# Six of the twelve modulation sums of each layer computed beside the mixer's first projections, the others moved from routing into the pair stage

## The chip, the cores and the metric

The kernel runs on one core of one Trainium2 chip, in one launch. The metric is the device time of the launch in microseconds (us). A launch of the kernel before takes 3448.68 us (median of three, 3448.21 to 3457.46). The execution that was profiled took 3438.13 us, of which the trace spans 3436.4 us. PE is the matrix engine, PEld its weight loads, DVE the vector engine, ACT the scalar engine, POOL the GpSimd engine and SP the engine that issues nearly all DMAs.

## The reference

The program is a two-layer trunk over 512 tokens of width 1024. Each layer is a mixer and a feed-forward part with product-key experts, both in float32, and both are steered by a vector `c` of the sequence:

```python
for l in range(DEPTH):
    mod = c_act @ ada_w[l] + ada_b[l]                 # 6144 numbers
    sh1, sc1, g1, sh2, sc2, g2 = jnp.split(mod, 6, axis=-1)
    h = modulate(rmsnorm(x, ln1_g[l]), sh1, sc1)      # h * (1 + sc1) + sh1
    proj = h @ w_full
    r, k, v, wd, ad, gd = ...                         # token shift, split
    y_rwkv = rwkv7_mix(...)                           # a recurrence over tokens
    y_pool = multiscale_pool(...)
    x = x + g1 * (concatenate([y_rwkv, y_pool]) @ w_out[l])
    h2 = modulate(rmsnorm(x, ln2_g[l]), sh2, sc2)
    x = x + g2 * peer_ffn(h2, ...)                    # 16 queries, top 16, experts
return rmsnorm(x, lnf_g)
```

`mod` is a product of one vector with a matrix of 1024 x 6144. The kernel computes it in 12 groups of 512 columns per layer: groups 0 to 3 are `sh1` and `sc1`, 4 and 5 are `g1`, 6 to 9 are `sh2` and `sc2`, and 10 and 11 are `g2`. So a layer's groups 0 to 3 are wanted before its mixer begins, 4 and 5 before its output projection, 6 to 9 before its queries, and 10 and 11 at the layer's end.

## The kernel before, in words

**A group's sum.** A group reads 2 MB of `ada_w`. DVE multiplies eight tiles of 128x512 by a column each and adds them up (one TENSOR_SCALAR, L195, and seven SCALAR_TENSOR_TENSOR, L197, in `ada_acc`). `ada_mod` then sums the accumulator over its partitions with four matmuls of one column (L205) into a PSUM tile of the ring `pss`, which has two slots, and DVE adds the bias (L207). Four of the groups also cost a tiny `mod_scale` on DVE.

**Where the tiles land.** With `early=True` the group's data come as eight loads of 256 KB into general buffers (L183). Otherwise they come as four loads of 512 KB into the ring `raw` (L185), which has three buffers. The same ring carries the weights: `split_next` loads a weight tile into `raw` (L257), ACT copies its upper part (L259), DVE subtracts to get the lower part (L260), and `mm3` runs three passes of eight matmuls with the two parts. Weights are split three tiles ahead of their use. SP issues loads in program order, so a load that waits for a buffer holds up the loads behind it.

**The stages of a layer.** The mixer projects tile 12, the four k tiles 4 to 7, then four r tiles, tile 13, four v tiles and four pooled tiles (`shifted` evacuates the first ten; L384 on ACT, L385 on DVE). Between them come decay, normalisation and the scaled keys (`at`, L435 and following), whose products go through DRAM into `Ai`. A triangular solve on DVE (L479 to L484) turns `Ai` into `Fi`, and the result goes through DRAM into `Fb`. The pair stage begins where `Fb` is first used (L644): chunks of the recurrence for four pairs of heads, with a chain of small steps between PE and DVE (L706 to L708), ending in the output projection. Then the feed-forward part runs 16 query projections (evacuated on ACT, L916), each followed by scores whose best 16 are found on DVE (L903 to L908, L930). The rest of routing sorts out experts, and one-hot products (L1044) and the dense expert loops follow.

**Who sets the order.** A scheduler fixes each engine's order of instructions before the launch, starting from the order of the calls. `zipped` and `blend` deal out lists of steps among each other. `tc.issue_after(x)` keeps what is called within it behind the instruction `x` on the same engine; nothing else binds these sums to a place.

**Where the sums stand.** `ADA_MIX` names those in the pair stage (three of its `zipped` calls carry `ada` steps). `ADA_PRE` names those among the queries and scores: every second query starts one of its list with `early=True`. Groups 0 to 3 of layer 0 are summed at the very start of the program, and no edit touches them.

Of the kernel before, what the change touches and what calls it, by code (L numbers as in the profile page):

```python
# [9 lines left out]
F32 = mybir.dt.float32  # L10
# [4 lines left out]
AF = mybir.ActivationFunctionType  # L15
ALU = mybir.AluOpType
# [3 lines left out]
P = 128  # L20
T = 512
# [3 lines left out]
L = 2  # L25
# [9 lines left out]
SPILL = 88  # L35
GPRE = 24
GFRAC = 0.0
ADA_MIX = [[(l, g) for g in range(4, 10)] for l in range(L)]
ADA_PRE = [[(0, 10), (0, 11), (1, 0), (1, 1), (1, 2), (1, 3)], [(1, 10), (1, 11)]]
ADA_DENSE = [[], []]  # L40
SIDES, NPRE = (0, 8, 0, 3), 2
APER, AOFF, ADEL = 2, 1, 4
# [66 lines left out]
def body(ctx, tc, A, tap=None):  # L109
    nc = tc.nc  # L110
    V, S, G, TE = nc.vector, nc.scalar, nc.gpsimd, nc.tensor
# [3 lines left out]
    st = ctx.enter_context(tc.tile_pool(name="st", bufs=3))  # L115
# [7 lines left out]
    def nm(p):  # L123
        cnt[0] += 1
        return f"{p}{cnt[0]}"
# [3 lines left out]
    def bank(shape=(P, T)):  # L129
        return psp[0].tile(list(shape), F32, tag="ps", name=nm("ps"))  # L130

    def sbank(shape=(P, T)):
        return pss.tile(list(shape), F32, tag="pss", name=nm("pss"))

    def s2t(name, shape=(P, T), dt=F32):
        return s2.tile(list(shape), dt, tag="s2", name=nm(name))
# [6 lines left out]
    sc_ = pers.tile([P, ND], F32, name="silu_c")  # L143
# [5 lines left out]
    def C(n):  # L149
        o, w = COFF[n]  # L150
        return const[:, o:o + w]
# [21 lines left out]
    A2 = [pers.tile([P, ND], F32, name=f"A2_{l}") for l in range(L)]  # L173

    first = {}

    def ada_acc(l, g, side=0, early=False):
        acc = s2t("acc")
# [23 lines left out]
    def ada_mod(l, g, acc):  # L202
        pt = sbank((P, 4))
        for m in range(4):
            TE.matmul(pt[:, m:m + 1], acc[:, m * P:(m + 1) * P], C("one"), start=True, stop=True)  # L205
        o = VOFF["adab"][0]
        V.tensor_tensor(mods[l][:, 4 * g:4 * g + 4], pt, vecs[l][:, o + 4 * g:o + 4 * g + 4], op=ALU.add)  # L207
        if g in (2, 3, 8, 9):
            mod_scale(l, 1 if g < 6 else 2, g % 2)
# [21 lines left out]
    def vec(l, n, i=0, w=1):  # L231
        o = VOFF[n][0]
        return vecs[l][:, o + i:o + i + w]

    def mod_scale(l, which, half):
        a, ln, off = (A1, "ln1", 8) if which == 1 else (A2, "ln2", 32)
        o = 4 * half
        V.scalar_tensor_tensor(a[l][:, o:o + 4], mods[l][:, off + o:off + o + 4], 1.0, vec(l, ln, o, 4), op0=ALU.add, op1=ALU.mult)
# [24 lines left out]
    def weights(*key):  # L263
        i = taken[0]
        assert seq[i] == key, (seq[i], key)
        taken[0] += 1
        while len(ready) < min(i + WAHEAD, len(seq)):
            split_next()
        w, ready[i] = ready[i], None
        return w  # L270
# [47 lines left out]
    def mixer(l):  # L318
        with ExitStack() as mctx:
# [26 lines left out]
            omu = m.tile([P, 15], F32, name="omu")  # L346
# [24 lines left out]
            def project(n):  # L371
                if n in begun:
                    w, pt = begun.pop(n)
                    mm3(pt, w, hs, range(ND // 2, ND), start=False)
                    return pt
                w = weights(f"w_in{l}", n)
                pt = sbank()
                mm3(pt, w, hs)
                return pt

            def shifted(n, out):
                pt = project(n)
                mi = n if n < 14 else 14
                S.activation(out, pt, AF.Identity, scale=omu[:, mi:mi + 1])  # L384
                V.scalar_tensor_tensor(out[:, 1:], pt[:, :T - 1], vec(l, "mu", mi), out[:, 1:], op0=ALU.mult, op1=ALU.add)  # L385
                return out

            def c3(z):
# [2 lines left out]
            def n3(z):  # L391
                return z.rearrange("p (n t) -> p n t", n=NT)

            lora = shifted(12, s2t("lora"))
            wda = s2t("wda")
            V.memset(wda[64:65, :], 1.0)
            S.activation(wda[0:64], lora[0:64], AF.Tanh)
            sig = []
            for t in range(NT):
                pt = bank()  # L400
# [4 lines left out]
            for p in range(4):  # L405
                pt = bank()
                TE.matmul(pt, sm[64:128, SM_AUP + p * P:SM_AUP + (p + 1) * P], lora[64:128], start=True, stop=True)
                bt_[p] = s2t("bt")
                S.activation(bt_[p], pt, AF.Sigmoid, bias=vec(l, "a0", p))
            ks = [shifted(4 + p, s2t("k")) for p in range(4)]  # L410

            Pds, kps = [], ks
# [23 lines left out]
            for p in range(4):  # L436
                k, a, at, Pd, Pi = ks[p], bt_[p], at_[p], Pds[p], kt_[p]
# [312 lines left out]

            todo, accs = ADA_MIX[l], {}

            def ada_step(i):
                if i > 0:
                    ada_mod(*todo[i - 1], accs.pop(i - 1))
                if i < len(todo):
                    with tc.issue_after(beat[0].ins):
                        accs[i] = ada_acc(*todo[i])

            ada = [lambda i=i: ada_step(i) for i in range(len(todo) + 1)]  # L760
# [24 lines left out]
            for n in range(ND):  # L785
                xr = s2t("x")
                nc.sync.dma_start(xr, A["xT"][:, n] if l == 0 else xs[n])
                if n in held:
                    w, pt = held.pop(n)
                    mm3(pt, w, ys, (3,), True, start=False)  # L790
                else:
                    w, pt = weights("w_out", l, n), (sbank, bank)[n % 2]()
# [10 lines left out]
            pt = sbank((P, 2, NT))  # L803
# [10 lines left out]
    def peer(l):  # L814
        with ExitStack() as pctx:
# [73 lines left out]
            with ExitStack() as rctx:  # L889
# [159 lines left out]

                pre = list(ADA_PRE[l])  # L1050
                for hp in range(16):
# [204 lines left out]
    for l in range(L):  # L1256
        mixer(l)
        peer(l)
# [56 lines left out]
```

## Time and profile before

| what | value |
|---|---|
| median of three launches | 3448.68 us |
| the profiled execution | 3438.13 us |
| its span in the trace | 3436.4 us |
| mean granted PE clock | 0.952 of full speed |
| PE busy | 3211.2 us (93%) |
| DVE busy | 2809.3 us (82%) |
| ACT busy | 1386.0 us (40%) |
| modulation loads in the ring `raw` | 48 of 512 KB |
| modulation loads in general buffers | 96 of 256 KB |

The profiled execution is 10.55 us below the median, and 10.08 us below the fastest of the three launches. Busy shares are averages over stages that have different limits, so the profile is read by stretches. In layer 0 the front of the mixer is 62.0 to 225.3 us, the pair stage 225.3 to 442.5, the queries with their scores 442.5 to 577.8, the rest of routing 577.8 to 677.1, and the first part with one-hot products 677.1 to 1002.9. In layer 1 the same stretches begin at 1741.6, 1922.1, 2139.1, 2255.7 and 2356.4 us. The pair stage is read below up to 422.5 and 2119.0 us; what follows it up to the first query is the norm of the second half.

### The profile page before, as it was taken

How to read it: one execution, taken by the hardware profiler on the slowest of the kernel's cores; microseconds unless marked ns; L12 is line 12 of the kernel's file. 1: busy time of each engine (PE TensorE's matmuls, PEld its weight loads, DVE VectorE, ACT ScalarE, POOL GpSimd, SP SyncE). 2: the span in 40 equal slices, each digit the busy share in tenths (PEclk: the TensorE clock that was granted, in tenths of full speed). 3: DMA queues.
4: the chain of work that ended last, by engine and by line, in shares of the span. 5: the costliest groups of instructions: out<-in, count | busy, mean ns of one | idle time of the engine just before them, and what ended most of it. 6: DMA issues, size and time to landing. Idle time of an engine off the chain costs nothing. (4 is left out here: it accounts for less than half of the span.)

```text
span 3436.4 us, 51106 instructions
## 1 busy us (share of the span) xinstructions
PE 3211.2 (93%) x18154; PEld 2814.1 (82%) x18154; DVE 2809.3 (82%) x6227; ACT 1386.0 (40%) x2228; POOL 875.7 (25%) x684
## 2 busy tenths in 40 slices
PE   5889888999999999999899898999999999999997
PEld 3777678999998888888777777889999888888886
DVE  5677499989868888899939675999997688888998
ACT  3433222446563334333353323334656533333333
POOL 2000001432202222555500000023240122245564
PEclk7989899999999999999999888999999999999998
DMA  5214253567789999999922233345767999999996
GB/s 196 77 47 144 88 176 122 171 228 257 262 310 344 345 343 342 350 377 398 356 72 82 79 111 117 99 134 180 275 237 282 333 334 343 342 340 335 362 392 237
DMA packets 361377, 826.41 MB, mean 240 GB/s; under 512 B 46496, under 2 KB 189600, under 8 KB 357792
## 3 DMA queue, kind: packets, MB, share of 16 engines
q1 hardware_dynamic: 287392, 554.68, 47.5%
q0 software_dynamic: 73728, 268.47, 20.8%
q8 instruction: 142, 2.33, 0.3%
q14 instruction: 115, 0.94, 0.1%
HBM read 730.75 MB, written 92.27 MB: 240 GB/s over the span
## 5 line engine op out<-in xcount | busy, mean ns | idle before, releaser
L277 PE MATMUL pss<-hi,wsp 128*128 128x384 f32 (+1 forms) x5168 | 1081.5, 360 | 88.4 <-DVE wsp L260 27.8
L1162 PE MATMUL ps<-vv,wg 128*128 128x512 f32 x4608 | 1077.3, 392 | 22.7 <-DVE vv L1146 6.9
L277 PEld LDWEIGHTS pss<-hi,wsp 128*128 128x128 f32 x5168 | 941.0, 195 | 162.8 <-DVE wsp L260 39.9
L1162 PEld LDWEIGHTS ps<-vv,wg 128*128 128x128 f32 x4608 | 866.0, 189 | 208.0 <-ACT vv L1145 10.4
L259 ACT ACTIVATE wsp<-raw 128x1024 fp32r<-128x1024 f32 x341 | 360.0, 1057 | 548.5 <-PE pss L277 428.9
L277 PE MATMUL pss<-lo,wsp 128*128 128x384 f32 (+1 forms) x2584 | 534.1, 347 | 0.0
L855 POOL DMA_INDIRECT row<-u,ex x256 | 318.8, 1245 | 837.1 <-DVE row L861 639.5
L260 DVE TENSOR_TENSOR wsp<-raw,wsp 128x1024 fp32r<-128x1024 f32 x341 | 432.4, 1269 | 69.9 <-ACT wsp L259 69.7
L277 PEld LDWEIGHTS pss<-lo,wsp 128*128 128x128 f32 x2584 | 461.4, 188 | 22.2 <-issue 0.5
L855 POOL DMA_INDIRECT row<-v,ex x256 | 336.3, 1314 | 244.5 <-DVE ox L869 190.6
L1146 DVE TENSOR_TENSOR vv<-raw,vv 128x512 fp32r<-128x512 f32 x512 | 345.4, 692 | 43.1 <-ACT vv L1145 39.3
L1145 ACT ACTIVATE vv<-raw 128x512 fp32r<-128x512 f32 x512 | 291.4, 619 | 111.5 <-DMA raw<-v 76.9
L1136 ACT ACTIVATE wg<-ge 128x384 fp32r<-128x384 f32 x256 | 132.9, 524 | 497.6 <-DVE ge L1134 206.3
L861 DVE SCALAR_TENSOR_TENSOR row<-row,hx 128x1024 f32<-128x1024 f32 x256 | 318.4, 1250 | 14.0 <-DMA row<-u,ex 14.0
L869 DVE SCALAR_TENSOR_TENSOR ox<-row,wx,ox 128x1024 f32<-128x1024 f32 x254 | 325.3, 1281 | 2.4
L971 POOL TENSOR_TENSOR eq<-eq,cid 128x400 f32<-128x400 f32 x128 | 181.7, 1439 | 478.8 <-DVE eq L969 341.1
L937 POOL TENSOR_TENSOR hf<-hi,lo 128x128 f32<-128x128 f32 x16 | 7.8, 503 | 925.6 <-DVE tw L906 450.4
L1137 DVE TENSOR_TENSOR wg<-ge,wg 128x384 fp32r<-128x384 f32 x256 | 141.3, 555 | 104.6 <-ACT wg L1136 93.9
L1046 ACT ACTIVATE gb<-ps 128x512 f32<-128x512 f32 x192 | 199.0, 1161 | 0.0
L1134 DVE TENSOR_TENSOR ge<-ge,g 128x192 f32<-128x192 f32 x496 | 157.0, 353 | 46.3 <-DMA g<-gscr 39.3
L1129 ACT ACTIVATE ge<-pss 128x384 f32<-128x384 f32 x80 | 39.2, 490 | 249.0 <-PE pss L277 243.1
L1025 DVE TENSOR_TENSOR oh<-oh,selg 128x1024 f16<-128x1024 f16 x96 | 71.2, 742 | 44.9 <-PE ps L1044 44.7
(459 smaller groups left out, 3194.5 us busy)
## 6 DMA issues: line engine op xcount, KB each, us to landing
raw<-uT SPq DMA_DIRECT2D x256, 512.0 KB
raw<-v SPq DMA_DIRECT2D x256, 512.0 KB
gscr<-gb SPq DMA_DIRECT2D x24, 2048.0 KB
g<-gscr SPq DMA_DIRECT2D x124, 384.0 KB
gespill<-ge SPq DMA_DIRECT2D x176, 192.0 KB
ge<-gespill SPq DMA_DIRECT2D x176, 192.0 KB
ada<-ada SPq DMA_DIRECT2D x96, 256.0 KB
raw<-ada SPq DMA_DIRECT2D x48, 512.0 KB
```

Of the source, the lines that this page charges most:

```text
L259: S.activation(w[:, 0], raw, AF.Copy)
L260: V.tensor_tensor(w[:, 1], raw, w[:, 0].bitcast(F32), op=ALU.subtract)
L277: TE.matmul(pt, w[:, a, k * P:(k + 1) * P], hs[k][b], start=start and n == 0, stop=stop and n == len(steps) - 1)
L855: G.indirect_dma_start(out=rows[n], out_offset=None, in_=A["u" if n < P else "v"], in_offset=bass.IndirectOffsetOnAxis(ap=ex[:, n % P:n % ...
L861: V.scalar_tensor_tensor(row, row, 1.0, hx, op0=ALU.mult, op1=ALU.mult, accum_out=dots[:, e:e + 1])
L869: V.scalar_tensor_tensor(ox, row, wx[:, e:e + 1], ox, op0=ALU.mult, op1=ALU.add)
L971: pace["G"] = G.tensor_tensor(eq, eq, z["id"][:, h].unsqueeze(1).to_broadcast([P, 8, NC]), op=ALU.mult)
L1046: S.activation(gb[:, :, o:o + 4].rearrange("p i t -> p t i"), pt, AF.Copy, scale=1.0 / GSC)
L1134: V.tensor_tensor(gq, gq, g[:, :, c % IG], op=ALU.mult)
L1145: S.activation(vv[0][q], raw[:, q * T:(q + 1) * T], AF.Copy)
L1146: vlo[q] = V.tensor_tensor(vv[1][q], raw[:, q * T:(q + 1) * T], vv[0][q].bitcast(F32), op=ALU.subtract)
L1162: end[0] = TE.matmul(acc[t][d2], wg[a][:, ts_], vv[b][d2], start=(c == 0 and a == 0 and b == 0), stop=(c == NK - 1 and a == 1))
```

## The change

Groups 4 to 9 of each layer go from the pair stage into `ADA_FRONT`. `ada_parts` cuts each group into five steps: four quarters (one load of 512 KB into the ring `raw` and two operations on DVE each) and `ada_mod`. That makes 30 steps per layer. `shifted` evacuates a projection and then calls `FSTEPS` = 3 of them, held behind its own evacuation on ACT, which binds none of the engines that the steps use. The ten calls of `shifted` for tiles 12, 4 to 7, 0 to 3 and 13 therefore use up the 30 steps. The places in the pair stage take over what stood among the scores: six groups in layer 0 (its own 10 and 11, and 0 to 3 of layer 1), and two in layer 1. Routing gets none. The number of groups, their operations and their bytes stay as they were; eight groups that used loads of 256 KB now use loads of 512 KB in the ring.

```diff
-ADA_MIX = [[(l, g) for g in range(4, 10)] for l in range(L)]
-ADA_PRE = [[(0, 10), (0, 11), (1, 0), (1, 1), (1, 2), (1, 3)], [(1, 10), (1, 11)]]
+ADA_FRONT = [[(l, g) for g in range(4, 10)] for l in range(L)]
+ADA_MIX = [[(0, 10), (0, 11), (1, 0), (1, 1), (1, 2), (1, 3)], [(1, 10), (1, 11)]]
+ADA_PRE = [[], []]
+FSTEPS = 3
...
+    def ada_parts(l, g):
+        accs = []
+
+        def quarter(q):
+            if q == 0:
+                accs.append(s2t("acc"))
+            w = st.tile([P, 2, T], F32, tag="raw", name=nm("raw"))
+            nc.sync.dma_start(w, A["ada"][l, g, q])
+            for kk in range(2):
+                k = 2 * q + kk
+                if k == 0:
+                    V.tensor_scalar(accs[0], w[:, kk], sc_[:, k:k + 1], None, op0=ALU.mult)
+                else:
+                    V.scalar_tensor_tensor(accs[0], w[:, kk], sc_[:, k:k + 1], accs[0], op0=ALU.mult, op1=ALU.add)
+
+        return [lambda q=q: quarter(q) for q in range(4)] + [lambda: ada_mod(l, g, accs[0])]
...
+            front = [f for lg in ADA_FRONT[l] for f in ada_parts(*lg)]
+
             def shifted(n, out):
                 pt = project(n)
                 mi = n if n < 14 else 14
-                S.activation(out, pt, AF.Identity, scale=omu[:, mi:mi + 1])
+                begin = S.activation(out, pt, AF.Identity, scale=omu[:, mi:mi + 1])
                 V.scalar_tensor_tensor(out[:, 1:], pt[:, :T - 1], vec(l, "mu", mi), out[:, 1:], op0=ALU.mult, op1=ALU.add)
+                with tc.issue_after(begin.ins):
+                    for _ in range(FSTEPS):
+                        if front:
+                            front.pop(0)()
                 return out
```

The lines move down by up to 25: the sums of the front stand at L186 (load), L190 and L192 (DVE) afterwards, L257 becomes L276, L260 becomes L279, L479 and L480 become L504 and L505, and L903 to L906 become L928 to L931.

On SP, the issue order in layer 0 before the solve, just ahead of and behind the first `acmp` store to DRAM. Before:

```order
L257 DMA raw_981<-w_in 128x1024
L257 DMA raw_1023<-w_in 128x1024
L257 DMA raw_1066<-w_in 128x1024
L465 DMA ascr_124<-acmp_646 32x16x32 x4
L257 DMA raw_1109<-w_in 128x1024
L257 DMA raw_1150<-w_in 128x1024
L465 DMA ascr_124<-acmp_647 32x16x32 x4
```

The same place after:

```order
L186 DMA raw_903<-ada 128x1024
L186 DMA raw_907<-ada 128x1024
L186 DMA raw_911<-ada 128x1024
L490 DMA ascr_124<-acmp_715 32x16x32 x4
L276 DMA raw_929<-w_in 128x1024
L490 DMA ascr_124<-acmp_716 32x16x32 x4
L186 DMA raw_961<-ada 128x1024
L186 DMA raw_972<-ada 128x1024
L493 DMA Ai<-ascr_124 128x1024
```

The loads of the sums now take two or three buffers of the ring between two weight tiles, and two of them stand ahead of the load of `Ai`.

On DVE, the small rows of the solve in layer 0 (`Fi`, `Ai`), with the splits of weights (`wsp`) among them. Before:

```order
L479 TENSOR_TENSOR prod<-Fi,Ai 128x36 x2
L480 TENSOR_REDUCE Fi<-prod 128x6 x2
L479 TENSOR_TENSOR prod<-Fi,Ai 128x49 x2
L480 TENSOR_REDUCE Fi<-prod 128x7 x2
L479 TENSOR_TENSOR prod<-Fi,Ai 128x64 x2
L480 TENSOR_REDUCE Fi<-prod 128x8 x2
L260 TENSOR_TENSOR wsp_1152<-raw_1150,wsp_1152 128x1024
```

The same rows after:

```order
L279 TENSOR_TENSOR wsp_988<-raw_986,wsp_988 128x1024
L504 TENSOR_TENSOR prod<-Fi,Ai 128x36 x2
L192 SCALAR_TENSOR_TENSOR acc_971<-raw_1018,silu_c,acc_971 128x512
L505 TENSOR_REDUCE Fi<-prod 128x6 x2
L192 SCALAR_TENSOR_TENSOR acc_971<-raw_1018,silu_c,acc_971 128x512
L504 TENSOR_TENSOR prod<-Fi,Ai 128x49 x2
L192 SCALAR_TENSOR_TENSOR acc_971<-raw_1022,silu_c,acc_971 128x512
L505 TENSOR_REDUCE Fi<-prod 128x7 x2
L192 SCALAR_TENSOR_TENSOR acc_971<-raw_1022,silu_c,acc_971 128x512
L504 TENSOR_TENSOR prod<-Fi,Ai 128x64 x2
```

Where the steps of the solve followed each other, an operation of a sum now stands between them.

On DVE, the first score of layer 0, where `sc` are a query's scores. Before:

```order
L197 SCALAR_TENSOR_TENSOR acc_3342<-ada_3349,silu_c,acc_3342 128x512
L903 MAX SV_3260<-sc_3372 128x8
L197 SCALAR_TENSOR_TENSOR acc_3342<-ada_3350,silu_c,acc_3342 128x512
L904 MAX_INDEX si_3374<-SV_3260,sc_3372 128x8
L906 MATCH_REPLACE tw_3377<-SV_3260,sc_3372 128x128
L903 MAX SV_3261<-sc_3372 128x8
```

The same place after:

```order
L928 MAX SV_3400<-sc_3487 128x8
L929 MAX_INDEX si_3489<-SV_3400,sc_3487 128x8
L931 MATCH_REPLACE tw_3492<-SV_3400,sc_3487 128x128
L928 MAX SV_3401<-sc_3487 128x8
```

The operations of the sums are gone from between the scores.

## Rows read from the trace of the kernel before

**Rows 1.** The page: busy time, share and instructions of each engine.

```profile
PE 3211.2 (93%) x18154; PEld 2814.1 (82%) x18154; DVE 2809.3 (82%) x6227; ACT 1386.0 (40%) x2228; POOL 875.7 (25%) x684
```

**Rows 2.** Windows by stage: start:end, length, busy of each engine, PEclk, DMA share, GB/s.

```profile
62.00:225.30 163.30, 143.82 (x730) 116.29 (x730) 110.46 (x225) 68.19 (x115) 0.00 (x0) 0.91 0.26 75
225.30:422.50 197.20, 182.70 (x1476) 150.27 (x1474) 124.47 (x277) 62.12 (x128) 0.00 (x0) 0.85 0.30 97
442.50:577.80 135.30, 119.10 (x593) 102.35 (x593) 133.01 (x663) 38.88 (x55) 3.93 (x8) 0.92 0.44 145
577.80:677.10 99.30, 94.40 (x532) 91.35 (x531) 95.02 (x307) 37.41 (x50) 49.89 (x33) 1.00 0.55 165
...
1741.60:1922.10 180.50, 164.75 (x784) 130.31 (x784) 125.47 (x248) 74.98 (x125) 0.00 (x0) 0.90 0.23 70
1922.10:2119.00 196.90, 180.53 (x1474) 148.29 (x1473) 124.51 (x277) 62.01 (x128) 0.00 (x0) 0.88 0.30 97
2139.10:2255.70 116.60, 109.58 (x551) 94.06 (x551) 112.78 (x626) 38.21 (x55) 3.83 (x8) 0.96 0.31 97
2255.70:2356.40 100.70, 96.56 (x543) 95.08 (x541) 93.06 (x305) 37.40 (x50) 42.04 (x33) 0.98 0.54 163
```

**Rows 3.** The score stretches, sums' operations alone: busy of DVE, ACT, POOL.

```profile
442.50:577.80 135.30, 33.47 (x48) 0.00 (x0) 0.00 (x0) 0.92 0.44 145
2139.10:2255.70 116.60, 11.29 (x16) 0.00 (x0) 0.00 (x0) 0.96 0.31 97
```

**Rows 4.** Timeline of ACT, late queries of layer 1: start, duration, operation, idle before.

```profile
2219.88 0.60 ACT L916 ACTIVATE qT<-pss 128x512 f32<-128x512 f32 x1 [4.38 <-PE pss L277]
...
2226.23 0.60 ACT L916 ACTIVATE qT<-pss 128x512 f32<-128x512 f32 x1 [4.32 <-PE pss L277]
```

**Rows 5.** The sums' operations by line: duration in ns, min/median/max.

```profile
L197 DVE SCALAR_TENSOR_TENSOR acc<-raw,silu_c,acc x84: 700/745/753, 256.5 to 2043.8; 128x512 f32<-128x512 f32 x84
...
L195 DVE TENSOR_SCALAR acc<-raw,silu_c x12: 476/481/487, 253.5 to 2037.1; 128x512 f32<-128x512 f32 x12
```

**Rows 6.** Windows of DVE alone in the fronts, parted at the first `at`.

```profile
66.08:121.46 55.38, 16.38 (x23) 0.95 0.19 57
121.46:216.92 95.46, 89.09 (x193) 0.90 0.33 94
1750.92:1806.59 55.67, 16.68 (x24) 0.97 0.18 57
1806.59:1911.65 105.06, 97.55 (x207) 0.90 0.31 91
```

**Rows 7.** Timeline of DVE about the solve of layer 0.

```profile
144.69 2.35 DVE L260 TENSOR_TENSOR wsp<-raw,wsp 128x1024 fp32r<-128x1024 f32 x2
...
158.63 0.23 DVE L479 TENSOR_TENSOR prod<-Fi,Ai 128x1 f32<-128x1 f32 x2 [4.60 <-DMA Ai<-ascr]
...
174.38 0.74 DVE L385 SCALAR_TENSOR_TENSOR v<-pss,vec,v 128x511 f32<-128x511 f32 x1
...
216.17 0.75 DVE L589 TENSOR_TENSOR bk<-kt,PC 128x256 f32<-128x256 f32 x2
```

**Rows 8.** Waits in layer 1's pair stage: who for whom, us, times, longest.

```profile
DVE M L708 <- PE psc L706: 20.5, 18, 3.9
...
PE psc L706 <- DVE M L708: 7.6, 12, 3.6
```

**Rows 9.** Timelines of SP and DVE: a sum's load and the operation that waits for it.

```profile
257.30 3.56 SPq L185 DMA_DIRECT2D raw<-ada  x3
...
260.94 0.75 DVE L197 SCALAR_TENSOR_TENSOR acc<-raw,silu_c,acc 128x512 f32<-128x512 f32 x1 [0.43 <-DMA raw<-ada]
```

**Rows 10.** Timeline of PE: projections of layer 0 behind a wait and without one.

```profile
91.42 5.54 PE L277 MATMUL pss<-hi,wsp 128*128 128x512 f32 x16 [2.80 <-DVE k L385]
...
98.62 3.79 PE L277 MATMUL pss<-hi,wsp 128*128 128x512 f32 x16
...
175.17 6.57 PE L277 MATMUL pss<-hi,wsp 128*128 128x512 f32 x16 [9.87 <-DVE v L385]
```

## The prediction, made before the changed kernel had run

> **What bounds the kernel now.** I read the page's busy table first. PE works 93% of the span and DVE 82% [rows 1], so neither alone explains the time, and a change that moves DVE work needs the stages apart. I therefore cut the span into windows by stage [rows 2]. They show three kinds of stretch. In the queries and scores of layer 0, DVE is busy 133.01 of 135.30 us: it sets the end there, and PE, with 119.10, waits for it. In layer 1 the same stretch has DVE at 112.78 of 116.60. In the pair stage PE is busy 182.70 of 197.20 and DVE 124.47; in layer 1 180.53 and 124.51 of 196.90. There DVE has a third of its time free. In the front of the mixer PE leads on the average (143.82 of 163.30, with DVE at 110.46), but that average hides two parts. Parted at the first `at` row, DVE works 16.38 of 55.38 us ahead of it and 89.09 of 95.46 behind it, and in layer 1 16.68 of 55.67 and 97.55 of 105.06 [rows 6]. So the front begins with an idle DVE and ends in a solve that DVE alone sets, since the pair stage cannot begin before `Fi` is through.
>
> The price of the sums comes next. One accumulating operation is 0.745 us and the first of a group 0.481 [rows 5], so a group is 0.48 + 7 x 0.745 = 5.70 us of DVE. Among the scores they take 33.47 us in layer 0 (48 operations, six groups) and 11.29 in layer 1 (16, two groups) [rows 3].
>
> **Routing: what is removed.** The two layers do the same scores with different numbers of groups, so they measure the price on the path. The stretch is 135.30 - 116.60 = 18.70 us longer for 33.47 - 11.29 = 22.18 us more of sums, 0.84 us for each. The rest of routing is alike (99.30 and 100.70) [rows 2], so nothing is handed on. At 0.84, layer 0 loses 28.2 us and layer 1 9.5, and both come out at 107.1. Two floors lie near. DVE without the sums still needs 133.01 - 33.47 = 99.5 us and 112.78 - 11.29 = 101.5. PE's floor is read from the late queries of layer 1, behind the last sum: they follow each other by 2226.23 - 2219.88 = 6.35 us [rows 4], and sixteen of them with a last score of about the same length are 108. An estimate of 110 for both layers is the poor end (25 + 7 = 32 saved), and a DVE that never waits, at about 101, the good end (34 + 15 = 49). I take 0.84, the measured slope: 38 us saved.
>
> **Pair stage.** In layer 0 six groups stay six, at nothing. Layer 1 has four fewer, 22.8 us of DVE. DVE has 72.4 us free there [rows 2], and PE's matmuls wait for its chain step `M` only 7.6 us in 12 waits, while `M` waits for PE 20.5 us in 18 [rows 8]. The sums can have lengthened at most those 7.6 us and a share of other short waits. Between nothing and -12 I take -5. What hides the sums there is PE's own work; they stay hidden in layer 0.
>
> **Front, first half.** The ten calls take three steps each, so groups 4 to 6 are dealt out up to the fourth k tile and 7 to 9 on the r tiles and tile 13. Three groups, 17.1 us, fall into the stretch where DVE has 39 us free [rows 6]. They are not quite free of charge. A load of the ring took 260.94 - 257.30 = 3.64 us from its issue to its use [rows 9], and now the loads of the sums share three buffers with the weights: behind a full ring SP stops, and the next weight tile with it. On DVE an operation that waits for such a load holds up the splits and evacuations behind it, which PE waits for. And each group's column sums take one of two slots of the ring `pss`, between two projections. I charge less than one round trip, 1.5 us in layer 0 and 3 in layer 1, where the front carries one tile more and the stretch is as short. The bounds are nothing and three further round trips, 11 us.
>
> **Front, second half.** Here the other three groups, 17.1 us with 0.45 of bias additions, meet a DVE that is busy 93%. The order shows them among the small rows of the solve. With them comes work that stood earlier before: an evacuation and product of an r tile, 1.4 us (an evacuation is 0.74 [rows 7]), and two splits, 2.35 us [rows 7]. That is 21.3 us more in front of the last `bk` product, which ended the front's DVE work at 216.9 [rows 7]. Against it stands the idle time of that stretch: 6.4 us in layer 0, of which 4.60 is one wait for `Ai` [rows 7], and 7.5 in layer 1. Sums can fill it only where their loads have landed; I take half, 3.2 and 3.5. So layer 0 gets 21.3 - 3.2 + 1.5 = 19.6 us later, layer 1 21.3 - 3.5 + 3 = 20.8, together 40.4. The low ends fill all the idle time and leave the earlier work in its place (17.5 - 6.4 = 11 and 17.5 - 7.5 = 10); the high ends fill none and add 11 us of round trips (32 and 33). Nothing makes up for this behind the solve: PE has only the pair stage to go on with, and that waits for `Fb`.
>
> **The sum.** 40.4 - 38 - 5 = -2.6 us. The profiled execution took 3438.13 us (span 3436.4), so it would become 3435.5. The median of the runs shown is 10.55 us above the profiled execution; the same difference set against it gives 3446.1.
>
> **The rivals.**
>
> A, slower: SP paces the fronts. The order puts two sum loads ahead of the load of `Ai` and two or three between weight tiles. If the ring is full when SP comes to them, `Ai`'s load and the weights stand behind a buffer that DVE frees late, because DVE itself is at the solve or waits for a load. For it speaks that DVE already waited for such loads in the pair stage, where they have the ring nearly to themselves [rows 9]; against it, that 24 loads at (3.64 + 1.5) / 3 buffers fill 41 us of a front of 160. It decides from the point where a front stalls by three round trips beyond my charge: 10.9 us in each layer, 21.8 in all, 3468.
>
> B, faster: DVE's idle time in the second half is filled completely and the first half is free. Then the fronts cost 21.3 - 6.4 + 21.3 - 7.5 = 28.7; with scores nearer to the full DVE (42 saved) and 8 from the pair stage the sum is -21.3, 3427. For it speaks that the loads are independent of everything and can be early; against it, that the 4.60 us wait stands behind the very loads that SP would have to bring.
>
> C, the clock. PE's granted clock is lowest where it waits: 0.91 and 0.90 in the fronts, 0.85 and 0.88 in the pair stages, 0.98 to 1.00 in the later routing [rows 2]. Sixteen products took 3.79 us with no wait ahead, 5.54 behind a wait of 2.80 us and 6.57 behind one of 9.87 [rows 10], so a new wait is paid again, by 1.75 to 2.8 us. If each front gets five new ones with half of them on the path, that is 5 x 2.3 = 11 us: 3457. Against it speaks that the scores lose waits of the same kind at the same time.
>
> The Trainium skill, page "TensorE: Matmul & The Clock Gate", section "HAM oscillation — how this bites in real kernels", says that PE's idle gaps send its clock back to the half and that the loss recurs with every gap instead of being paid once. The trace agrees in direction, by 5.54 and 6.57 us against 3.79 [rows 10]. By that rule the change, which trades waits in a stage that PE is slowed in for DVE time in a stage at 0.92 and 0.96, comes out as rival C does, 3457.
>
> That the change does not do what it says is excluded: its order shows no sum among the scores.
>
> **How the numbers follow.** A measurement of this kernel can tell about 0.3% (10.3 us) from no change. Forecast: 0.35, with its own range 3434 to 3458 (faster 0.08, same 0.24, slower 0.03). A: 0.23 (same 0.01, slower 0.22). B: 0.30 (faster 0.27, same 0.03). C: 0.12 (same 0.07, slower 0.05). Together faster 0.35, same 0.35, slower 0.30. The gain in routing is well bounded and the cost of the fronts badly, from 21 to 65 us, so the sum runs from 21 - 49 - 12 = -40 to 65 - 32 = +33. Cases A and B lie inside, and 3420 to 3473 leaves out their outer halves.
>
> **What would show it.** Routing: the stretch from first query to last score should be about 107 us in both layers, and DVE busy about 100. Pair stages: 197 us again in layer 0 and about 192 in layer 1. Fronts: the first `at` at most 3 us later than 121.5 and 1806.5 on their stage's own scale, the first use of `Fb` about 20 us later in each layer, and DVE close to full between the two. If `at` is late by more than 3 us or the load of `Ai` waits, A holds. If the first use of `Fb` is late by under 15 us, B holds. A granted clock of the fronts well under 0.90, with products at 5.5 to 6.6 us for sixteen behind new waits, would be C. The forecast is wrong altogether if the scores keep 115 us or more without any sums, which would make PE their bound, or if the fronts do not lengthen at all.

## The result and the profile after

The changed kernel takes 3480.99 us (median of four launches, 3473.15 to 3486.19) against 3448.44 for the kernel before on the same chip: ratio 1.0106, 95% interval 1.0083 to 1.0130. That is slower by about one per cent and above the forecast range of 3420 to 3473 us. The profiled execution has a span of 3482.0 us, 45.6 more than before.

The stages, from the two traces. "Front" begins at the ACT evacuation of the lora projection (L384, now L405) and ends at the first use of `Fb` (L644, now L669). The pair stage, with the norm behind it, goes to the first query's evacuation (L916, now L941), the scores go to the start of the last L930 (now L955), and the rest to the next lora evacuation or the end of the span.

| us | layer 0 before | after | layer 1 before | after | forecast |
|---|---|---|---|---|---|
| front: lora to first `at` | 48.2 | 64.3 | 51.1 | 61.6 | +1.5, +3 |
| front: `at` to solve | 37.1 | 34.0 | 36.8 | 34.9 | } |
| front: solve | 48.4 | 69.2 | 58.5 | 81.5 | } +18.1, +17.8 |
| front: solve to `Fb` | 18.3 | 28.1 | 20.3 | 23.0 | } |
| pair stage | 217.2 | 225.7 | 217.0 | 213.5 | 0, -5 |
| scores | 135.2 | 107.2 | 116.4 | 107.3 | -28.2, -9.5 |
| rest | 1177.7 | 1178.3 | 1180.9 | 1180.6 | 0, 0 |

The windows of the kernel after, in the columns of [rows 2]: fronts, scores and the routing behind them.

```profile
62.00:268.40 206.40, 175.24 (x782) 136.15 (x782) 143.82 (x281) 69.52 (x115) 0.00 (x0) 0.80 0.39 120
494.10:601.40 107.30, 103.89 (x533) 89.99 (x533) 103.43 (x607) 37.95 (x55) 5.62 (x8) 0.98 0.27 84
601.40:702.50 101.10, 96.84 (x546) 95.22 (x545) 93.39 (x307) 37.50 (x50) 42.19 (x33) 0.98 0.53 164
1765.80:1980.60 214.80, 183.92 (x833) 143.60 (x833) 158.43 (x304) 75.92 (x124) 0.00 (x0) 0.82 0.38 118
2194.10:2301.60 107.50, 104.09 (x534) 90.12 (x534) 103.47 (x608) 37.98 (x55) 5.61 (x8) 0.98 0.27 85
```

The scores came out as forecast: 107 us in both layers, DVE at 103.4, at a granted clock of 0.98. The loss is in the fronts. Against [rows 2] the granted clock fell from 0.91 and 0.90 to 0.80 and 0.82, and DVE has 62.6 and 56.4 us idle there although it got 33 us more to do. So something other than DVE's load holds the fronts up. PE's timeline at the start of the front of layer 0 shows where it begins. Before, PE runs the second and third k projection (L277) while ACT and DVE prepare the lora product:

```profile
74.12 1.98 PE L277 MATMUL pss<-lo,wsp 128*128 128x512 f32 x8
75.94 3.79 PE L277 MATMUL pss<-hi,wsp 128*128 128x512 f32 x16
79.56 1.07 PE L277 MATMUL pss<-lo,wsp 128*128 128x512 f32 x4
80.47 3.60 PE L401 MATMUL ps<-sm,wda 65*128 65x512 f32 x8
```

After, nothing is left to run, and the second k projection (L296) starts at 87.71 behind the first group's column sums (L224):

```profile
76.86 7.20 PE L426 MATMUL ps<-sm,wda 65*128 65x512 f32 x8 [4.90 <-ACT wda L422]
83.98 2.07 PE L432 MATMUL ps<-lora,sm 64*128 64x512 f32 x2
85.98 1.86 PE L224 MATMUL pss<-const,acc 128*128 128x1 f32 x8
87.71 2.48 PE L296 MATMUL pss<-hi,wsp 128*128 128x512 f32 x5
```

The same eight matmuls took 3.60 us before and 7.20 behind the 4.90 us wait, twice as long: the upper and the lower of PE's two levels, 2.4 and 1.2 GHz. The Trainium skill, page "TensorE: Matmul & The Clock Gate", section "HAM oscillation — how this bites in real kernels", says of a kernel with waits between its products that the clock falls back at every such wait and the loss is paid each time instead of once; by these two rows the trace agrees. The window of that stretch, before and then after, with half the matmuls and a clock of 0.61:

```profile
66.08:97.30 31.22, 28.42 (x99) 19.94 (x98) 8.02 (x9) 14.33 (x19) 0.00 (x0) 0.91 0.23 67
66.08:97.30 31.22, 26.32 (x53) 13.20 (x52) 11.29 (x17) 10.74 (x15) 0.00 (x0) 0.61 0.36 119
```

The whole first half of layer 0, from the lora evacuation to the first `at`, before and then after:

```profile
73.30:121.50 48.20, 45.40 (x216) 35.45 (x215) 15.93 (x23) 32.02 (x48) 0.00 (x0) 0.96 0.22 66
72.80:137.10 64.30, 56.46 (x223) 40.02 (x224) 28.27 (x44) 30.10 (x45) 0.00 (x0) 0.79 0.41 131
```

It is 16.1 us longer. PE's time without work grew from 2.8 to 7.8 us, which is 5.0 of it. The other 11.1 us are busy time: about as many matmuls at a clock of 0.79 instead of 0.96. In layer 1 the 10.5 us are 1.4 of idle and 9.1 of busy time.

### The profile page after: what moved, and what is told of

It is laid out like the page before. It is cut to its first block, busy times and chain, and to the rows that moved or that the text cites. A ratio compares the mean times of both kernels' runs of the same rounds, so it can differ in the third digit from the quotient of the medians.

```text
span 3482.0 us, 51013 instructions
## 1 busy us (share of the span) xinstructions
PE 3245.2 (93%) x18154; PEld 2831.5 (81%) x18154; DVE 2812.7 (81%) x6227; ACT 1389.4 (40%) x2228; POOL 870.5 (25%) x684
## 5 line engine op out<-in xcount | busy, mean ns | idle before, releaser
L296 PE MATMUL pss<-hi,wsp 128*128 128x384 f32 (+1 forms) x5168 | 1069.9, 357 | 66.3 <-DVE wsp L279 28.1
L296 PEld LDWEIGHTS pss<-hi,wsp 128*128 128x128 f32 x5168 | 931.2, 193 | 140.4 <-DVE wsp L279 40.3
L296 PE MATMUL pss<-lo,wsp 128*128 128x384 f32 (+1 forms) x2584 | 533.7, 347 | 0.0
L279 DVE TENSOR_TENSOR wsp<-raw,wsp 128x1024 fp32r<-128x1024 f32 x341 | 429.0, 1258 | 66.2 <-ACT wsp L278 65.8
L296 PEld LDWEIGHTS pss<-lo,wsp 128*128 128x128 f32 x2584 | 461.5, 188 | 22.3
L996 POOL TENSOR_TENSOR eq<-eq,cid 128x400 f32<-128x400 f32 x128 | 174.0, 1379 | 485.0 <-DVE eq L994 346.6
L962 POOL TENSOR_TENSOR hf<-hi,lo 128x128 f32<-128x128 f32 x16 | 11.2, 726 | 969.8 <-DVE si L933 946.0
L1159 DVE TENSOR_TENSOR ge<-ge,g 128x192 f32<-128x192 f32 x496 | 156.9, 353 | 40.4 <-DMA g<-gscr 34.7
```

What stands on the lines that cost most here:

```text
L279: V.tensor_tensor(w[:, 1], raw, w[:, 0].bitcast(F32), op=ALU.subtract)
L296: TE.matmul(pt, w[:, a, k * P:(k + 1) * P], hs[k][b], start=start and n == 0, stop=stop and n == len(steps) - 1)
L996: pace["G"] = G.tensor_tensor(eq, eq, z["id"][:, h].unsqueeze(1).to_broadcast([P, 8, NC]), op=ALU.mult)
L1159: V.tensor_tensor(gq, gq, g[:, :, c % IG], op=ALU.mult)
```

## The experiments

The stage lengths of all runs from their traces, in us, layer 0 / layer 1:

| kernel | lora to `at` | solve | front | pair | scores |
|---|---|---|---|---|---|
| before | 48.2 / 51.1 | 48.4 / 58.5 | 152.0 / 166.7 | 217.2 / 217.0 | 135.2 / 116.4 |
| after | 64.3 / 61.6 | 69.2 / 81.5 | 195.6 / 201.0 | 225.7 / 213.5 | 107.2 / 107.3 |
| no loads in front | 61.6 / 59.4 | 68.2 / 79.5 | 190.1 / 199.9 | 214.6 / 209.7 | 107.3 / 107.3 |
| loads only in front | 62.1 / 58.4 | 64.3 / 78.1 | 179.9 / 194.1 | 221.4 / 213.5 | 107.2 / 107.3 |
| general buffers, POOL | 76.4 / 71.3 | 75.9 / 90.1 | 213.0 / 220.0 | 214.5 / 213.5 | 107.3 / 107.3 |
| all in the pair stage | 48.2 / 54.1 | 48.3 / 58.6 | 151.8 / 169.8 | 253.6 / 230.6 | 107.3 / 107.3 |
| ring of five | 53.3 / 54.9 | 70.0 / 78.9 | 177.6 / 189.8 | 220.9 / 213.6 | 107.2 / 107.4 |
| late column sums | 55.0 / 51.8 | 70.3 / 85.4 | 177.9 / 191.3 | 217.4 / 214.4 | 107.3 / 107.3 |
| late, six steps a call | 75.1 / 76.1 | 49.8 / 64.7 | 179.3 / 197.2 | 227.5 / 221.9 | 107.2 / 107.3 |
| among the one-hot products | 49.2 / 53.9 | 48.1 / 58.6 | 158.8 / 169.5 | 212.3 / 220.4 | 107.2 / 107.3 |
| ring of five, loads only | 53.5 / 53.5 | 58.9 / 68.6 | 172.0 / 184.6 | 217.1 / 217.1 | 107.2 / 107.2 |
| ring of five, no loads | 50.5 / 58.1 | 60.5 / 69.5 | 164.0 / 183.9 | 217.7 / 212.8 | 107.2 / 107.3 |
| three groups in front | 57.0 / 58.1 | 47.9 / 57.9 | 161.0 / 169.3 | 227.4 / 217.4 | 119.9 / 107.2 |
| two groups in front | 51.5 / 51.1 | 49.8 / 57.0 | 155.3 / 162.2 | 227.6 / 224.2 | 125.2 / 107.3 |

My first theory was the ring: the sums' loads take the buffers of the weights (theory R). Its rival was that DVE's operations are the whole cost (theory D).

**No loads in the front.**

```diff
-            w = st.tile([P, 2, T], F32, tag="raw", name=nm("raw"))
-            nc.sync.dma_start(w, A["ada"][l, g, q])
+            w = const[:, 0:T].unsqueeze(1).to_broadcast([P, 2, T])
```

> The sums of the fronts multiply a resident constant instead of loaded columns, so the loads of those 12 groups are left out and all 96 operations on DVE stay. In the changed kernel the time from the evacuation of the lora projection to the first at is 64.3 us in layer 0 and 61.6 in layer 1 (48.2 and 51.1 before), and to the first use of Fb 195.6 and 201.0 (152.0 and 166.7 before). Theory R (the shared ring starves PE of weights): the first at comes back to within 3 us of before in both layers, PE's granted clock in that stretch to 0.93 or more, and the fronts take at most 172 and 187 us; total about 3435 to 3445. Theory D (DVE's operations are the cost, wherever the data come from): the fronts stay above 188 and 195, total above 3465.

3474.07 us, ratio 1.0079 (1.0053 to 1.0105). Without a single load in the ring, `at` is still 13.4 and 8.3 us late. Theory R explains at most 3 us of the first half, and every figure lies where theory D put it.

**Loads only.**

```diff
-V.scalar_tensor_tensor(accs[0], w[:, kk], sc_[:, k:k + 1], accs[0], ...)
+V.scalar_tensor_tensor(accs[0][:, 0:16], w[:, kk, 0:16], sc_[:, k:k + 1], accs[0][:, 0:16], ...)
```

> All loads of the fronts stay in the shared ring, but each of the 84 accumulating operations works on 16 columns instead of 512, so most of the sums' arithmetic is left out (about 0.15 us instead of 0.745 each). Theory R: the first at is still 8 us or more late in both layers, because what matters is the ring and SP's order, and the fronts take at least 172 and 182 us. Theory D: the fronts come back to 152 and 167 within 5 us, total about 3411 (before less the 37 us that routing gave).

3463.30 us, ratio 1.0044 (1.0026 to 1.0062). An operation on 16 columns took 0.234 us, not 0.15, so the sums still take 11.9 of 33.0 us in each front. With a third of the arithmetic, `at` is late by 13.9 and 7.3 us. So theory D is wrong for the first half too: this run alone speaks for R (whose 8 us layer 1 misses by 0.7), the one before it alone for D, and what both kernels have in common is something else.

**Data in general buffers, loaded by POOL.**

```diff
-            w = st.tile([P, 2, T], F32, tag="raw", name=nm("raw"))
-            nc.sync.dma_start(w, A["ada"][l, g, q])
+            w = [s2t("ada") for _ in range(2)]
+            for kk in range(2):
+                nc.gpsimd.dma_start(w[kk], A["ada"][l, g, q, :, kk])
```

> The same sums at the same places, with their data in the general buffers as loads of 256 KB, issued by POOL, which is idle in the mixer, so that neither the ring nor SP is shared. Theory R: first at within 3 us of before, fronts about 172 and 187 (20 us each of DVE in the second half remain), total about 3440. Theory D: no change against the changed kernel, 3475 to 3486.

3517.03 us, ratio 1.0202 (1.0178 to 1.0226): worse than both theories said. The general buffers come round late, as POOL's waits in the front of layer 0 show (who for whom, us, times, longest):

```profile
POOL ada L187 <- DVE acc L193: 53.1, 4, 50.6
```

It shows that another place for the data is no cure, and no more about the cause.

**All in the pair stage.**

```diff
-ADA_FRONT = [[(l, g) for g in range(4, 10)] for l in range(L)]
-ADA_MIX = [[(0, 10), (0, 11), (1, 0), (1, 1), (1, 2), (1, 3)], [(1, 10), (1, 11)]]
+ADA_FRONT = [[], []]
+ADA_MIX = [[(0, g) for g in range(4, 12)] + [(1, g) for g in range(4)], [(1, g) for g in range(4, 12)]]
```

> No sums in the fronts and none among the scores: 12 groups in the pair stage of layer 0 and 8 in that of layer 1. Scores at 107 us in both layers as in the changed kernel (37 less than before), fronts as before. Theory H (PE bounds the pair stage, DVE's free 72 us hide the sums): the pair stages take 217 to 225 us and the total is about 3415 to 3425. Theory C (DVE's small chain steps stand behind the sums): at 12 groups DVE is full, pair 0 takes 240 us or more, and the total is 3435 or more.

3454.53 us, ratio 1.0034 (1.0015 to 1.0054). Six further groups in layer 0 (34 us of DVE) cost 36 us there, and two in layer 1 cost 13.6, while the four that the change took out of it gave back 3.5. The first groups nearly hide in the pair stage and the next do not. The times are those of theory C, but not its mechanism: DVE was not full, and PE's waits for the chain step `M` in layer 0 take 10.1 us instead of 8.4. The pair stage of layer 0, before and then in this kernel:

```profile
225.30:442.50 217.20, 199.15 (x1546) 163.79 (x1544) 137.45 (x297) 69.39 (x140) 0.00 (x0) 0.85 0.32 105
226.70:480.30 253.60, 229.27 (x1594) 189.38 (x1592) 168.18 (x353) 69.36 (x140) 0.00 (x0) 0.78 0.40 131
```

PE's idle time grew by 6 us and its busy time by 30, for 48 small matmuls more, at a clock of 0.78 instead of 0.85. Most of the 36 us are thus in products at the lower clock; what lowered it is not shown.

**The turn in the PSUM ring.** What the first two kernels have in common with the changed one is PE's order. Its piece behind the lora products:

```
49 L432 MATMUL ps_456<-lora_409,sm 128x512
50 L224 MATMUL pss_491<-const,acc_424 128x1 x4
51 L296 MATMUL pss_508<-hi_241,wsp_236 128x512 x2
```

`pss_491` is group 4's column sum, `pss_508` the second k projection. The ring `pss` has two slots, given out in the order of the calls, and here, as in the rows of the result, the projection stands behind the column sum, which needs all eight operations of its group. This made theory P, with Q as its rival.

```diff
-        return [lambda q=q: quarter(q) for q in range(4)] + [lambda: ada_mod(l, g, accs[0])]
+        return [lambda q=q: quarter(q) for q in range(4)] + [lambda: ada_mod(l, g, accs[0], bank)]
...
-    def ada_mod(l, g, acc):
-        pt = sbank((P, 4))
+    def ada_mod(l, g, acc, ring=None):
+        pt = (ring or sbank)((P, 4))
```

> One edit to the changed kernel: the column sums of the fronts' groups (the four small matmuls of ada_mod) write to the PSUM ring of five tiles instead of the ring pss of two, which the projections take in turn. Theory P (a group's column sums take their turn in pss ahead of the next projection, so PE cannot run projections ahead until all eight operations of the group are through): first at after the lora evacuation at most 52 us in layer 0 and 55 in layer 1 (64.3 and 61.6 in the changed kernel, 48.2 and 51.1 before), PE's granted clock there 0.9 or more, fronts about 172 and 187 us with the DVE time of the second half left over, total 3440 to 3452. Theory Q (it is the amount of DVE work and the ring of loads, not the turn in pss): first at still over 57 us, fronts over 185 and 193, total over 3465.

3463.13 us, ratio 1.0070 (1.0052 to 1.0088). The first `at` comes at 53.3 and 54.9 us, the fronts lose 18.0 and 11.2 us against the changed kernel. PE again runs the projections ahead, with the upper clock for the same eight matmuls:

```profile
73.96 1.98 PE L296 MATMUL pss<-lo,wsp 128*128 128x512 f32 x8
75.78 3.79 PE L296 MATMUL pss<-hi,wsp 128*128 128x512 f32 x16
79.40 1.52 PE L296 MATMUL pss<-lo,wsp 128*128 128x512 f32 x6
80.76 3.60 PE L426 MATMUL ps<-sm,wda 65*128 65x512 f32 x8
...
88.39 1.05 PE L224 MATMUL ps<-const,acc 128*128 128x1 f32 x8
```

```profile
66.08:97.30 31.22, 28.74 (x104) 20.51 (x103) 18.05 (x26) 13.07 (x19) 0.00 (x0) 0.89 0.43 145
```

PE does 104 matmuls in the 31.22 us in which the changed kernel did 53, at a clock of 0.89 instead of 0.61. The first half of layer 0 as a whole:

```profile
73.10:126.40 53.30, 50.82 (x247) 40.31 (x246) 29.13 (x45) 27.92 (x42) 0.00 (x0) 0.94 0.47 158
```

PE is without work for 2.5 us there, and the clock is back at 0.94 (1.00 in layer 1). These are the rows of theory P and not of Q, though `at` misses P's 52 us in layer 0 by 1.3. The total is above the range I gave: the fronts keep 25.6 and 23.1 us over before instead of 20 each, and the pair stage of layer 0 and the rest were longer by 3.7 to 5.3 us each in this trace.

The second way to free the turn leaves the sums in the fronts and moves the column sums into the pair stage:

```diff
+    owed = []
...
-        return [...] + [lambda: ada_mod(l, g, accs[0])]
+        return [...] + [lambda: owed.append((l, g, accs[0]))]
...
             def ada_step(i):
+                for _ in range(-(-len(owed) // (len(todo) + 1 - i))):
+                    ada_mod(*owed.pop(0))
```

> The sums stay in the fronts, but their column sums and bias additions move into the pair stage; the accumulators wait in general buffers. Theory P: as with the ring of five, first at at most 52 and 55 us, fronts about 172 and 187, pair stages as in the changed kernel plus at most 3 us, total 3440 to 3452. Theory Q: first at over 57 us, total over 3465.

3462.24 us, ratio 1.0059 (1.0036 to 1.0083): by another edit nearly the same fronts, 177.9 and 191.3 us (`at` in layer 0 is 3 us beyond P's bound, and the solve of layer 1 is 6.5 us longer than with the ring of five). Theory P stands on two kernels, with two limits. By the ratios the freed turn is worth 0.36 and 0.47 of 1.06 per cent, and the intervals meet at their ends, so the proof lies in the fronts. And for the first half it is firm in layer 0 alone. There three traces of the changed kernel give 64.3 to 69.6 us, and no kernel with the turn freed and three steps a call is over 57.0. In layer 1 the three traces give 61.6, 60.2 and 56.6, while kernels with the turn freed give 51.1 to 58.1.

**Six steps a call.** The same kernel with `FSTEPS = 6`:

> As the kernel with late column sums, but six steps per call instead of three, so that all six groups are dealt out by the last k tile, where DVE stood idle for 39 us before. Theory P with room in that idle time: fronts about 160 and 175 us (8 over before), total 3418 to 3432, faster than both kernels. Rival: 24 loads ahead of the weights in the shared ring starve the projections, first at over 58 us, and the total is over 3450.

3480.56 us, ratio 1.0106 (1.0083 to 1.0130). The rival holds: the solve is back at 49.8 and 64.7 us (48.4 and 58.5 before), but `at` is 27 and 25 us late. Now the ring does starve the projections, as the waits of the first half of layer 0 say:

```profile
ACT wsp L279 <- DMA raw<-w_in: 24.5, 4, 11.1
```

So DVE's 39 idle us ahead of `at` are not free room: what is put there has to come through the ring in which the weights come.

**Among the one-hot products.** The kernel before, its groups of `ADA_PRE` handed to the third `blend` of routing instead of to every second query (`early=True` as before).

> The kernel before with one edit: its groups among the scores (six in layer 0, two in layer 1) move on to the one-hot products behind them, where PE is busy 314 of 326 us and DVE 281. Theory H (an engine off the path hides the sums): scores 107 us in both layers, the stretch of the one-hot products within 5 us of 326 and 323, total 3405 to 3418. Theory C (DVE's order delays what PE waits for, as in the pair stage): the rest of the layer takes 20 us or more longer in layer 0, total 3435 or more.

3480.40 us, ratio 1.0115 (1.0083 to 1.0148). The rest of layer 0 takes 1236.8 us instead of 1177.7, 59 us for 33.5 us of sums. The times are those of theory C; which wait makes 59 of it I have not separated. From 552.2 to 980.0 us the sums on DVE wait 13.3 us for their loads, and PE's weight loads 8.4 us for the bias additions that free a tile of `pss`, so the turn is a rival here as well.

**The second half, in parts.** On the kernel with the ring of five, the two cuts again: operations on 16 columns, and no loads.

> The kernel with column sums in the ring of five, with most of the fronts' arithmetic left out: each of the 84 accumulating operations works on 16 columns instead of 512. Theory A (in the second half the DVE time of the sums is the cost): the solve, 70.0 and 78.9 us with the arithmetic, comes back to 48 to 54 and 58 to 64, the fronts to 160 and 174 or less, total under 3430. Theory B (the loads in the shared ring and late projections stretch the solve): it stays above 64 and 74.

> The same kernel with the fronts' loads left out instead: the sums multiply a resident constant, all 96 operations stay. Theory A: the solve keeps 66 to 72 and 75 to 82 us, the first at comes to within 2 us of 48.2 and 51.1 (53.3 and 54.9 with loads). Theory B: the solve comes back to under 56 and 66 us.

3435.07 us (ratio 0.9979, 0.9957 to 1.0002) and 3430.25 us (0.9964, 0.9937 to 0.9990). The solve is 10.5 and 10.1 us longer than before with the loads and a third of the arithmetic, 12.1 and 11.0 with the arithmetic alone, and 21.6 and 20.4 with both. Neither theory A nor B is right; each has half. The windows of the solve in layer 0, with the instructions of the sums only (accumulators, `acc`; PE, PEld, DVE, ACT, POOL), ring of five, then no loads, then loads only:

```profile
164.40:234.40 70.00, 2.52 (x22) 2.63 (x21) 10.17 (x14) 0.00 (x0) 0.00 (x0) 0.99 0.47 150
```

```profile
159.60:220.10 60.50, 5.28 (x24) 5.19 (x24) 10.43 (x15) 0.00 (x0) 0.00 (x0) 0.88 0.21 68
```

```profile
165.50:224.40 58.90, 1.89 (x16) 2.09 (x16) 2.53 (x10) 0.00 (x0) 0.00 (x0) 1.00 0.48 163
```

Ten of the 17.6 us of sums that I had put behind the first `at` lie inside the solve, the other seven ahead of it. The other half are the projections. The same windows with the instructions on split weights (`wsp`; PE, PEld, DVE, ACT), before, ring of five, no loads and loads only:

```profile
158.60:207.00 48.40, 32.80 (x132) 26.23 (x130) 6.09 (x5) 5.28 (x5) 0.86 0.21 71
```

```profile
164.40:234.40 70.00, 52.05 (x218) 40.61 (x218) 12.23 (x10) 10.56 (x10) 0.99 0.47 150
```

```profile
159.60:220.10 60.50, 31.89 (x140) 25.76 (x138) 7.34 (x7) 5.30 (x6) 0.88 0.21 68
```

```profile
165.50:224.40 58.90, 50.38 (x211) 38.91 (x210) 11.03 (x9) 10.55 (x10) 1.00 0.48 163
```

With the loads in the ring, 211 to 218 products of projections fall into the solve, without them 140, before 132. The loads push three to four tiles of 24 products, with their splits and evacuations on DVE, from the stretch ahead of the solve into it. In the changed kernel, where the column sums still take their turn in `pss`, the loads are not needed for that. There the same count is 247, and 247 without loads too:

```profile
171.10:240.30 69.20, 60.85 (x247) 48.83 (x248) 12.18 (x10) 11.27 (x11) 0.93 0.47 153
170.50:238.70 68.20, 58.45 (x247) 47.08 (x248) 10.98 (x9) 10.17 (x10) 0.93 0.23 78
```

So either of the two, the turn or the loads, makes these projections late.

**Fewer groups in front.** Ring of five, and three groups (or two) in each front; what does not fit goes to the pair stage (six, five in layer 1 with three in front) and the rest to the scores of layer 0:

```diff
+ADA_FRONT = [[(l, g) for g in range(4, 7)] for l in range(L)]
+ADA_MIX = [[(0, 7), (0, 8), (0, 9), (0, 10), (0, 11), (1, 0)], [(1, g) for g in range(7, 12)]]
+ADA_PRE = [[(1, 1), (1, 2), (1, 3)], []]
```

> Column sums in the ring of five and only three groups in each front (4 to 6), where DVE stood idle ahead of the first at. Six groups in the pair stage of layer 0, five in that of layer 1, three among the scores of layer 0, none among those of layer 1. By the rows so far: fronts 5 and 4 us over before (152.0 and 166.7), pair stages as before, scores 135.2 - 3 x 4.7 = 121 and 107: 9 - 14 - 9 = -14, ratio to before about 0.996. If the first half is not as cheap once nothing follows it (fronts 10 us or more over before), the ratio is 0.999 or more.

> The same with two groups in each front (4 and 5), six in each pair stage, four among the scores of layer 0 and none in layer 1. Fronts 3 us over before each, scores 126 and 107, pair stages as before: 6 - 9 - 9 = -12, ratio about 0.9965. If a group in the front costs as much as in the changed kernel (7.2 and 5.7 us each), the ratio is 1.002.

3442.31 us (ratio 0.9985, 0.9966 to 1.0004) and 3442.99 us (0.9999, 0.9974 to 1.0023). Neither can be told from the kernel before. The scores gave back what was expected (15.3 + 9.2 and 10.0 + 9.1 us), the fronts took 9.0 + 2.6 with three groups and 3.3 - 4.5 with two, and the pair stage of layer 0 was 10 us longer in both traces (that of layer 1 by 7.2 with two groups). Of the versions that do all of the work, none beats the kernel before by more than can be measured.

**The same two kernels again.** Two more traces of each, since the pair stage of layer 0 was part of the miss.

> The kernel before, unchanged, for a second trace. If stage lengths belong to the order of instructions, the pair stages are 217.2 and 217.0 us within 1.5 us and the fronts 152.0 and 166.7. If they depend on the execution, a pair stage differs by 5 us or more.

> The changed kernel, unchanged, for a second trace. If its order makes the pair stage of layer 0 longer: 224 to 227 us again, fronts 195.6 and 201.0 within 2 us. If the execution does: 215 to 220 us at least once in the two repeats.

> The kernel before, unchanged, for a third trace: pair stages 217.2 and 217.0 us within 1.5 us if the order sets them, 5 us or more apart from that if the execution does.

> The changed kernel, unchanged, for a third trace: pair stage of layer 0 224 to 227 us again if the order sets it, 215 to 220 at least once in the two repeats if the execution does.

Single launches of 3447.14 and 3459.26 us (before) and 3488.50 and 3499.53 (after). The pair stage of layer 0 took 217.2, 219.4 and 223.7 us before, and 225.7, 226.7 and 222.5 after. The ranges overlap and one program shows 6.5 us of spread; that the difference of the averages, 5 us (220.1 and 225.0), belongs to the order is not shown. The windows of that stage in the two repeats of the kernel before:

```profile
230.00:449.40 219.40, 201.28 (x1546) 165.43 (x1544) 137.34 (x297) 69.50 (x141) 0.00 (x0) 0.84 0.31 104
226.30:450.00 223.70, 205.17 (x1546) 167.71 (x1544) 137.51 (x297) 69.39 (x140) 0.00 (x0) 0.82 0.31 102
```

With the first trace's 217.2 us PE is without work for 18.1, 18.1 and 18.5 us. What differs is its busy time, at clocks of 0.85, 0.84 and 0.82. The fronts are firm for the size of their change: 152.0, 155.3, 151.9 and 166.7, 168.5, 169.6 before, 195.6, 200.7, 196.4 and 201.0, 200.4, 197.0 after. The scores agree within 1.6 us. The rest of layer 0 does not: 1177.7, 1176.3 and 1188.8 us before, 1178.3, 1179.0 and 1192.6 after.

## Why the prediction was wrong, point by point

- **Routing** was right: 28.0 and 9.1 us saved against 28.2 and 9.5. Two layers with different numbers of groups gave the slope, and it carried over to none at all.
- **Pair stage**: layer 1 gave 3.5 us back for 22.8 us of DVE against 5. Layer 0 was forecast at nothing and took 8.5 more in the first trace; three traces of each leave it open whether any of that is the change's.
- **Front, first half, is the step that failed.** I named the column sums' turn in `pss` and charged them, with the ring, 1.5 and 3 us. Measured were 16.1 and 10.5. The price was taken from the transfer, a round trip of 3.64 us [rows 9], where the order mattered: PE's projections ahead came to stand behind a sum of eight operations, PE went idle, and its clock went to the lower level. The idle time is the smaller part, 5.0 and 1.4 us, and slower products the larger, 11.1 and 9.1. Freeing the turn took 18.0 and 11.2 us from the whole fronts; with the turn free, the first half costs 5.1 and 3.8 us. In layer 1 three traces of each kernel put the cost at 7 us on the average instead of 10.5.
- **Front, second half** was too low as well, 27.5 and 23.8 us against 18.1 and 17.8, and wrong in its make-up. With the turn free, the whole fronts are 25.6 and 23.1 us longer against the 19.6 and 20.8 forecast, and the solve 21.6 and 20.4; that this lies near is luck. I had 21.3 us of DVE time there, nearly all of it sums. The runs show about ten of sums and about ten of projections that came late, by the loads or by the turn.
- **The rivals.** A named the ring and SP's order, and its sign, `at` more than 3 us late, came true. But the run without loads contradicts it for the first half, so that sign did not tell the ring from the turn; the place it named is real in the second half and with six steps a call. Rival C's price, a wait paid again in slow products, is in the rows (3.60 and 7.20 us) and is the larger part of the first half, but it follows from the PE order: with the turn free the lora product shows neither the wait nor the slow matmuls. C charged 11 us for both fronts, and the first halves alone show 20. B fell with the first half.
- **The sum**: 43.6 + 34.3 for the fronts, + 8.5 - 3.5 for the pair stages, - 28.0 - 9.1 for the scores is + 45.8, and the spans differ by 45.6. The forecast had 40.4 - 5 - 38. Of the 48 us between them, 22 are the first half, 15 the second and 10 the pair stages.

## What to carry to other kernels

Before a small product is put among large ones, ask which ring its result takes its turn in. Here a tile that waits for slow work, in a ring of two, stopped products behind it that could have run ahead, and PE's lower clock then cost more than the wait itself (11.1 us against 5.0 in layer 0). Idle time of an engine is not yet room: what is put there must get its inputs without taking buffers from the engine that sets the end. That another way for the inputs would do is not shown; the one run that had it, with general buffers and POOL, kept the turn and was slower still. Where two layers do the same stage with different loads, their difference is the best price there is; where no row shows an edit's price, look in the built order for what it stands in front of.

## What the runs showed of the hardware

One and the same program differs from launch to launch by more than 30 us here. On one chip 34 of 35 launches of the kernel before lie between 3427.20 and 3464.53 us; the granted clock was 0.954 in the first of these two and 0.948 in the second. Three traces of it differ by 12.5 us in the rest of layer 0 (1176.3 to 1188.8) and by 6.5 in the pair stage of layer 0 (217.2 to 223.7), where PE's idle time is the same within 0.5 us and its clock is not. The eight matmuls of the lora product took 3.60 us where PE had not waited for them. Behind a wait of 4.90 us in layer 0 they took 7.20 in all three traces of the changed kernel. Behind the same wait of 2.49 or 2.50 us in layer 1 they took 7.20, 4.84 and 4.87 in the three: all eight were slow (1061 ns instead of 592), or only the last three.
